# Grouped instance normalisation in 4 MB tiles: statistics by sum and square instead of BN_STATS, coefficients for pairs of tiles

## The chip, the cores and the metric

The kernel runs on one core of one Trainium2 chip. The metric is device time in microseconds (us), the median of several executions of the whole kernel. For the kernel before it is 634.74 us over 12 runs, from 634.29 to 635.12 us.

Five engines of the core matter here. TensorE (PE) does small matrix products, VectorE (DVE) and ScalarE (ACT) do the work on the data, GpSimd (POOL) sets up constants, and SyncE (SP) only issues transfers. Transfers are carried by 16 DMA engines that all queues share.

## The reference

```python
B, G, C_per_g, H, W = 4, 8, 16, 256, 256
def reference(x, gamma):
    mu = x.mean(axis=(3, 4), keepdims=True)
    var = ((x - mu) ** 2).mean(axis=(3, 4), keepdims=True)
    x_norm = (x - mu) / np.sqrt(var + 1e-5)
    out = x_norm * gamma[None, :, :, None, None]
    return out.astype(np.float32)
```

There are 4 x 8 x 16 = 512 channels of 65,536 float32 numbers each. Every channel gets its own mean and variance, and every number of it becomes `x * scale + shift`, with scale = gamma / sqrt(var + 1e-5) and shift = -mean * scale. All of x has to be read before its channel can be written. In all 134.22 MB are read and 134.22 MB are written.

## The kernel before

**Units.** A channel is cut into S = 4 rows of F = 16384 numbers, and each row lies in one partition, so 128 partitions hold K = 32 channels: a unit of 8 MB. There are U = 16 units. A unit is loaded as two tiles (NCK = 2) of 128 x 8192 numbers, 4 MB each; in memory the rows of a tile are 32 KB long and start 64 KB apart. The pool `data` has six tiles (line 40), so three units are resident.

**Loads.** `load(u)` (lines 47 to 53) issues both transfers of a unit on SyncE's queue. Units 0 and 1 are loaded at once (line 55), unit u + 1 at the head of the loop's pass u. A load into a tile that has been used waits on SyncE until the store of that tile's old content is complete.

**Statistics.** `stats(u)` runs 32 BN_STATS of 512 columns on VectorE (line 94). `finalize` (lines 100 to 133) joins them with one BN_AGGREGATE (line 102), makes mean and mean square per partition, averages the four partitions of each channel with a matrix product on TensorE against the constant `avg` (line 109), and then makes nmean, var, std (Sqrt on ScalarE, line 125), rstd, scale and shift (lines 114 to 132), each a small instruction on 128 partitions.

**Normalising and storing.** `emit` (lines 135 to 141) normalises each of the two tiles in place on ScalarE (line 138) and issues its store on ScalarE's queue (line 141).

**Order.** The order is written out by hand: `manual_schedule` leaves each engine's instructions as the program lists them, and each engine works its own list in order, waiting on semaphores where its data comes from elsewhere. The loop is

```python
st0 = stats(0)
for u in range(1, U):
    if u + 1 < U:
        tiles[u + 1] = load(u + 1)
    st = stats(u)
    if u == 1:
        emit(0, *finalize(0, st0))
    emit(u, *finalize(u, st))
```

so `finalize(0)` stands behind `stats(1)` in VectorE's list, and in every later pass a unit's statistics, coefficients and stores follow each other.

Of the kernel before, what the change touches and what calls it, by code (L numbers as in the profile page):

```python
# [1 line left out]

# [4 lines left out]

F32 = mybir.dt.float32
ALU = mybir.AluOpType
ACTF = mybir.ActivationFunctionType  # L10


@with_exitstack
def kernel(
    ctx: ExitStack,
    tc: tile.TileContext,
    x: bass.AP,
    gamma: bass.AP,
    out: bass.AP,
):  # L20
    nc = tc.nc
    B, G, C, H, W = x.shape
    P = nc.NUM_PARTITIONS
    HW = H * W
    n_ch = B * G * C
    S = 4
    K = P // S
    F = HW // S
    U = n_ch // K
    CW = 8192  # L30
    NCK = F // CW
    FMAX = 512
    NG = (G * C) // K
    assert HW % S == 0 and F % CW == 0 and (G * C) % K == 0

    xv = x.rearrange("b g c h w -> (b g c h w)").rearrange("(u p f) -> u p f", p=P, f=F)
    ov = out.rearrange("b g c h w -> (b g c h w)").rearrange("(u p f) -> u p f", p=P, f=F)
    gv = gamma.rearrange("g c -> (g c)")

    data = ctx.enter_context(tc.tile_pool(name="data", bufs=3 * NCK))  # L40
    singles = ctx.enter_context(tc.tile_pool(name="singles", bufs=1))
    stats_pool = ctx.enter_context(tc.tile_pool(name="stats", bufs=2))
    psum = ctx.enter_context(tc.tile_pool(name="psum", bufs=2, space=bass.MemoryType.PSUM))

    ctx.enter_context(tc.manual_schedule())

    def load(u):
        ts = []
        for j in range(NCK):
            t = data.tile([P, CW], F32, name="xt")  # L50
            nc.sync.dma_start(out=t[:], in_=xv[u, :, j * CW : (j + 1) * CW])  # L51
            ts.append(t)
        return ts

    tiles = {0: load(0), 1: load(1)}


    g_row = singles.tile([1, G * C], F32, name="g_row")
    nc.scalar.dma_start(out=g_row[:], in_=gv[None, :])
    eps_t = singles.tile([P, 1], F32, name="eps_t")  # L60
    nc.vector.memset(eps_t[:], 1e-5)  # L61
    avg = singles.tile([P, K, S], F32, name="avg")
    nc.gpsimd.memset(avg[:], 1.0 / S)  # L63
    nc.gpsimd.affine_select(  # L64
        out=avg[:], in_=avg[:], pattern=[[-S, K], [0, S]], compare_op=ALU.is_ge,
        fill=0.0, base=0, channel_multiplier=1,
    )
    nc.gpsimd.affine_select(  # L68
        out=avg[:], in_=avg[:], pattern=[[S, K], [0, S]], compare_op=ALU.is_ge,
        fill=0.0, base=S - 1, channel_multiplier=-1,  # L70
    )
    one = singles.tile([1, 1], F32, name="one")
    nc.vector.memset(one[:], 1.0)
    g_rep = singles.tile([1, NG, K, S], F32, name="g_rep")
    nc.vector.tensor_copy(  # L75
        out=g_rep[:],
        in_=g_row[:].rearrange("o (n k) -> o n k", n=NG).unsqueeze(3).to_broadcast([1, NG, K, S]),
    )
    g_ps = psum.tile([P, NG], F32, name="g_ps")
    for n in range(NG):  # L80
        nc.tensor.matmul(  # L81
            out=g_ps[:, n : n + 1],
            lhsT=g_rep[:, n].rearrange("o k s -> o (k s)"),
            rhs=one[:],
            start=True, stop=True,
        )
    g_col = singles.tile([P, NG], F32, name="g_col")
    nc.vector.tensor_copy(out=g_col[:], in_=g_ps[:])  # L88

    def stats(u):  # L90
        st = stats_pool.tile([P, F // FMAX, 6], F32, name="st")
        for j in range(NCK):
            for s in range(CW // FMAX):
                nc.vector.bn_stats(  # L94
                    out=st[:, j * (CW // FMAX) + s, :],
                    in_=tiles[u][j][:, s * FMAX : (s + 1) * FMAX],
                )
        return st

    def finalize(u, st):  # L100
        mv = stats_pool.tile([P, 2], F32, name="mv")
        nc.vector.bn_aggr(out=mv[:], in_=st[:].rearrange("p n s -> p (n s)"))  # L102

        nc.vector.scalar_tensor_tensor(  # L104
            out=mv[:, 1:2], in0=mv[:, 0:1], scalar=mv[:, 0:1], in1=mv[:, 1:2],
            op0=ALU.mult, op1=ALU.add,
        )
        ps = psum.tile([P, 2], F32, name="ps")
        nc.tensor.matmul(  # L109
            out=ps[:], lhsT=avg[:].rearrange("p k s -> p (k s)"), rhs=mv[:],  # L110
            start=True, stop=True,
        )
        cm = stats_pool.tile([P, 2], F32, name="cm")
        nc.vector.tensor_copy(out=cm[:], in_=ps[:])  # L114
        nmean = stats_pool.tile([P, 1], F32, name="nmean")
        nc.vector.tensor_scalar(  # L116
            out=nmean[:], in0=cm[:, 0:1], scalar1=-1.0, scalar2=None, op0=ALU.mult,
        )
        var = stats_pool.tile([P, 1], F32, name="var")
        nc.vector.scalar_tensor_tensor(  # L120
            out=var[:], in0=cm[:, 0:1], scalar=nmean[:], in1=cm[:, 1:2],
            op0=ALU.mult, op1=ALU.add,
        )
        std = stats_pool.tile([P, 1], F32, name="std")
        nc.scalar.activation(out=std[:], in_=var[:], func=ACTF.Sqrt, bias=eps_t[:], scale=1.0)  # L125
        rstd = stats_pool.tile([P, 1], F32, name="rstd")
        nc.vector.reciprocal(out=rstd[:], in_=std[:])  # L127
        scale = stats_pool.tile([P, 1], F32, name="scale")
        g = u % NG
        nc.vector.tensor_mul(out=scale[:], in0=rstd[:], in1=g_col[:, g : g + 1])  # L130
        shift = stats_pool.tile([P, 1], F32, name="shift")
        nc.vector.tensor_mul(out=shift[:], in0=nmean[:], in1=scale[:])  # L132
        return scale, shift

    def emit(u, scale, shift):
        for j in range(NCK):
            t = tiles[u][j]
            nc.scalar.activation(  # L138
                out=t[:], in_=t[:], func=ACTF.Identity, bias=shift[:], scale=scale[:],
            )  # L140
            nc.scalar.dma_start(out=ov[u, :, j * CW : (j + 1) * CW], in_=t[:])


    st0 = stats(0)
    for u in range(1, U):
        if u + 1 < U:
            tiles[u + 1] = load(u + 1)
        st = stats(u)
        if u == 1:
            emit(0, *finalize(0, st0))  # L150
        emit(u, *finalize(u, st))
        del tiles[u - 1]


# [1 line left out]
_INS = ['x', 'gamma']  # L156
_OUTS = [((4, 8, 16, 256, 256), 'float32')]


# [23 lines left out]
```

## Time and profile before

| what | value |
|---|---|
| median of 12 runs | 634.74 us |
| the profiled execution's own time | 634.29 us |
| its span, first to last instruction | 632.6 us |
| VectorE busy | 343.3 us (54%), 644 instructions |
| ScalarE busy | 236.8 us (37%), 49 instructions |
| TensorE busy | 11.2 us (2%) |
| DMA, all queues | 268.50 MB, mean 424 GB/s over the span |
| one load, from issue to landing, median | 27.4 us |
| one store, from issue to landing, median | 50.7 us |

The page cuts the span into 40 equal slices of 15.8 us. A digit is the busy share of an engine in the slice in tenths, 9 meaning 90% or more; below it stands what the DMA engines moved. Queue q1 carries the loads issued by SyncE, q10 the stores issued by ScalarE, and q14 carries transfers of instructions. A group line names the source line, the engine, the operation, what is written and read, and how often; then busy time in us and mean ns of one; then the engine's idle time just before these instructions and what ended it. A suffix q (ACTq, SPq) marks the sequencer of an engine, which issues transfers without keeping the engine busy.

### The profile page before, as it was taken

How to read it: one execution, taken by the hardware profiler on the slowest of the kernel's cores; microseconds unless marked ns; L12 is line 12 of the kernel's file. 1: busy time of each engine (PE TensorE's matmuls, PEld its weight loads, DVE VectorE, ACT ScalarE, POOL GpSimd, SP SyncE). 2: the span in 40 equal slices, each digit the busy share in tenths (PEclk: the TensorE clock that was granted, in tenths of full speed). 3: DMA queues.
4: the chain of work that ended last, by engine and by line, in shares of the span. 5: the costliest groups of instructions: out<-in, count | busy, mean ns of one | idle time of the engine just before them, and what ended most of it. 6: DMA issues, size and time to landing. Idle time of an engine off the chain costs nothing.

```text
span 632.6 us, 972 instructions
## 1 busy us (share of the span) xinstructions
PE 11.2 (2%) x40; PEld 9.8 (2%) x40; DVE 343.3 (54%) x644; ACT 236.8 (37%) x49; POOL 1.4 (0%) x7
## 2 busy tenths in 40 slices
PE   1000000000000000000000000000000000000000
PEld 1000000000000000000000000000000000000000
DVE  2995486454765536665356653467535575354700
ACT  0004958053170622607135080440904408053180
POOL 0000000000000000000000000000000000000000
DMA  8998999999999999999999999999999999999996
GB/s 369 439 438 346 398 425 431 435 431 429 433 431 431 431 433 431 433 434 436 435 437 431 437 431 435 432 431 431 431 431 431 433 433 440 439 431 433 433 431 278
DMA packets 9226, 268.50 MB, mean 424 GB/s; under 512 B 1026, under 2 KB 1027, under 8 KB 1027
## 3 DMA queue, kind: packets, MB, share of 16 engines
q1 hardware_dynamic: 4608, 134.22, 49.4%
q10 hardware_dynamic: 4610, 134.22, 49.3%
q14 instruction: 8, 0.06, 0.0%
HBM read 134.22 MB, written 134.22 MB: 424 GB/s over the span
## 4 chain that ended last, share of the span: by engine, by line
DMA 60%; DVE 17%; another core or an unknown queue 12%; ACT 7%; PE 1%; issue 1%; SPq 0%; ACTq 0%
DMA xt<-in_x_dram 41%; DMA out_dram<-xt 19%; DVE st L94 14%; ACT xt L138 7%; DVE mv L102 1%; PE ps L109 1%; SPq L51 0%; DVE mv L104 0%; DVE var L120 0%; ACT std L125 0%; DVE cm L114 0%; DVE nmean L116 0%; DVE rstd L127 0%; DVE shift L132 0%
## 5 line engine op out<-in xcount | busy, mean ns | idle before, releaser
L94 DVE BATCH_NORM_STATS2 st<-xt 128x6 f32<-128x512 f32 x512 | 306.8, 677 | 219.4 <-DMA xt<-in_x_dram 219.2
L138 ACT ACTIVATE xt<-xt,shift,scale 128x8192 f32<-128x8192 f32 x32 | 230.8, 7213 | 16.7 <-DVE shift L132 9.9
L125 ACT ACTIVATE std<-var,eps_t 128x1 f32<-128x1 f32 x16 | 4.7, 295 | 359.6 <-DVE var L120 359.1
L109 PE MATMUL ps<-mv,avg 128*128 128x2 f32 x32 | 9.4, 362 | 584.2 <-DVE mv L104 584.2
L109 PEld LDWEIGHTS ps<-mv,avg 128*128 128x128 f32 x32 | 8.0, 311 | 585.5 <-DVE mv L104 536.1
L102 DVE BATCH_NORM_AGGREGATE mv<-st 128x2 f32<-128x192 f32 x16 | 16.3, 1021 | 0.5
L127 DVE RECIPROCAL rstd<-std 128x1 f32<-128x1 f32 x16 | 2.6, 164 | 18.6 <-ACT std L125 18.6
L114 DVE COPY cm<-ps 128x2 f32<-128x2 f32 x16 | 2.5, 159 | 10.9 <-PE ps L109 10.9
L120 DVE SCALAR_TENSOR_TENSOR var<-cm,nmean 128x1 f32<-128x1 f32 x16 | 3.5, 220 | 0.6
L104 DVE SCALAR_TENSOR_TENSOR mv<-mv 128x1 f32<-128x1 f32 x16 | 3.5, 219 | 0.6
L132 DVE TENSOR_TENSOR shift<-nmean,scale 128x1 f32<-128x1 f32 x16 | 2.6, 160 | 0.6
L130 DVE TENSOR_TENSOR scale<-rstd,g_col 128x1 f32<-128x1 f32 x16 | 2.5, 159 | 0.5
L116 DVE TENSOR_SCALAR nmean<-cm 128x1 f32<-128x1 f32 x16 | 2.5, 154 | 0.6
L81 PE MATMUL g_ps<-one,g_rep 1*128 1x1 f32 x8 | 1.9, 350 | 2.5 <-DVE g_rep L75 2.5
L81 PEld LDWEIGHTS g_ps<-one,g_rep 1*128 1x128 f32 x8 | 1.8, 322 | 2.5 <-DVE g_rep L75 2.5
L125 ACT ACT_TABLE_LOAD x1 | 1.3, 1283 | 1.3 <-PEq L167 1.3
L88 DVE COPY g_col<-g_ps 128x4 f32<-128x4 f32 x1 | 0.2, 162 | 2.0 <-PE g_ps L81 2.0
L75 DVE COPY g_rep<-g_row 1x512 f32<-1x512 f32 x1 | 0.4, 414 | 1.1 <-DMA g_row<-in_gamma_dram 1.1
L61 DVE MEMSET eps_t<- 128x1 f32 x1 | 0.1, 59 | 0.9 <-PEq L167 0.9
L64 POOL TENSOR_SCALAR_AFFINE_SELECT avg<-avg 128x128 f32<-128x128 f32 x1 | 0.5, 520 | 0.1
L68 POOL TENSOR_SCALAR_AFFINE_SELECT avg<-avg 128x128 f32<-128x128 f32 x1 | 0.5, 519 | 0.1
L63 POOL MEMSET avg<- 128x128 f32 x1 | 0.2, 205 | 0.3 <-POOLq L167 0.3
(5 smaller groups left out, 0.5 us busy)
## 6 DMA issues: line engine op xcount, KB each, us to landing
xt<-in_x_dram SPq DMA_DIRECT2D x32, 4096.0 KB, 27.4
out_dram<-xt ACTq DMA_DIRECT2D x32, 4096.0 KB, 50.7
g_row<-in_gamma_dram ACTq DMA_DIRECT2D x1, 0.5 KB
```

The lines of the kernel that those rows point to most:

```text
L81: nc.tensor.matmul(out=g_ps[:, n : n + 1], lhsT=g_rep[:, n].rearrange("o k s -> o (k s)"), rhs=one[:], start=True, stop=True,)
L94: nc.vector.bn_stats(out=st[:, j * (CW // FMAX) + s, :], in_=tiles[u][j][:, s * FMAX : (s + 1) * FMAX],)
L102: nc.vector.bn_aggr(out=mv[:], in_=st[:].rearrange("p n s -> p (n s)"))
L104: nc.vector.scalar_tensor_tensor(out=mv[:, 1:2], in0=mv[:, 0:1], scalar=mv[:, 0:1], in1=mv[:, 1:2], op0=ALU.mult, op1=ALU.add,)
L109: nc.tensor.matmul(out=ps[:], lhsT=avg[:].rearrange("p k s -> p (k s)"), rhs=mv[:], start=True, stop=True,)
L114: nc.vector.tensor_copy(out=cm[:], in_=ps[:])
L116: nc.vector.tensor_scalar(out=nmean[:], in0=cm[:, 0:1], scalar1=-1.0, scalar2=None, op0=ALU.mult,)
L120: nc.vector.scalar_tensor_tensor(out=var[:], in0=cm[:, 0:1], scalar=nmean[:], in1=cm[:, 1:2], op0=ALU.mult, op1=ALU.add,)
L125: nc.scalar.activation(out=std[:], in_=var[:], func=ACTF.Sqrt, bias=eps_t[:], scale=1.0)
L127: nc.vector.reciprocal(out=rstd[:], in_=std[:])
L132: nc.vector.tensor_mul(out=shift[:], in0=nmean[:], in1=scale[:])
L138: nc.scalar.activation(out=t[:], in_=t[:], func=ACTF.Identity, bias=shift[:], scale=scale[:],)
```

## The change

The unit becomes one tile: S = 8 rows of 8192 numbers per channel, K = 16 channels, U = 32 units of 4 MB, each contiguous in memory and moved by one transfer. Six tiles are resident as before, and all six are loaded at the start.

The statistics are a sum per partition on VectorE (`reduce_sum`) and a sum of squares on ScalarE (Square with an accumulator output; the squares themselves go to a byte tile `junk` that nobody reads). A matrix product with `navg` (-1/HW within each channel's eight partitions) gives minus the mean and minus the mean square in PSUM. Coefficients are made for two units together; the last two units are handled one by one. Of a pair, the first unit is normalised on VectorE and the second on ScalarE; of the last two units, 5376 columns on VectorE and 2816 on ScalarE. Stores stay on ScalarE's queue, after both normalisations of the pair, and each is followed in the program by the load of the unit six further on.

The diff, cut to its core; the constants' set-up moves from VectorE to GpSimd, and gamma is spread over eight columns instead of four.

```diff
-    S = 4
+    S = 8
...
-    CW = 8192
-    NCK = F // CW
-    FMAX = 512
     NG = (G * C) // K
+    AHEAD = 6
+    DV = 5376
...
-    data = ctx.enter_context(tc.tile_pool(name="data", bufs=3 * NCK))
+    data = ctx.enter_context(tc.tile_pool(name="data", bufs=AHEAD))
...
     def load(u):
-        ts = []
-        for j in range(NCK):
-            t = data.tile([P, CW], F32, name="xt")
-            nc.sync.dma_start(out=t[:], in_=xv[u, :, j * CW : (j + 1) * CW])
-            ts.append(t)
-        return ts
+        t = data.tile([P, F], F32, name="xt")
+        nc.sync.dma_start(out=t[:], in_=xv[u])
+        tiles[u] = t
-    tiles = {0: load(0), 1: load(1)}
+    for u in range(AHEAD):
+        load(u)
...
+    junk = singles.tile([P, F], U8, name="junk")
...
+    def coefficients(lo, n):
+        hi = lo + n
+        for u in range(lo, hi):
+            t = tiles[u]
+            nc.vector.reduce_sum(out=st[:, u, 0:1], in_=t[:], axis=AX.X)
+            nc.scalar.activation(
+                out=junk[:], in_=t[:], func=ACTF.Square, accum_out=st[:, u, 1:2],
+            )
+        ps = psum.tile([P, n, 2], F32, name="ps")
+        nc.tensor.matmul(
+            out=ps[:].rearrange("p n c -> p (n c)"), lhsT=navg_w,
+            rhs=st[:, lo:hi].rearrange("p n c -> p (n c)"), start=True, stop=True,
+        )
+        for i in range(n):
+            nc.vector.tensor_scalar(
+                out=nvar[:, lo + i : lo + i + 1], in0=ps[:, i, 0:1], scalar1=ps[:, i, 0:1],
+                scalar2=ps[:, i, 1:2], op0=ALU.mult, op1=ALU.add,
+            )
+        nc.scalar.activation(
+            out=std[:, lo:hi], in_=nvar[:, lo:hi], func=ACTF.Sqrt, bias=eps_t[:], scale=-1.0,
+        )
+        nc.vector.reciprocal(out=rstd[:, lo:hi], in_=std[:, lo:hi])
+        g = lo % NG
+        nc.vector.tensor_mul(out=scale[:, lo:hi], in0=rstd[:, lo:hi], in1=g_col[:, g : g + n])
+        nc.vector.tensor_mul(out=shift[:, lo:hi], in0=ps[:, :, 0], in1=scale[:, lo:hi])
+
+    def norm_vector(u, a, b):
+        t = tiles[u]
+        nc.vector.tensor_scalar(
+            out=t[:, a:b], in0=t[:, a:b], scalar1=scale[:, u : u + 1],
+            scalar2=shift[:, u : u + 1], op0=ALU.mult, op1=ALU.add,
+        )
+
+    def norm_scalar(u, a, b):
+        t = tiles[u]
+        nc.scalar.activation(
+            out=t[:, a:b], in_=t[:, a:b], func=ACTF.Identity,
+            bias=shift[:, u : u + 1], scale=scale[:, u : u + 1],
+        )
+
+    def store(u):
+        nc.scalar.dma_start(out=ov[u], in_=tiles.pop(u)[:])
...
+    for u in range(0, U - 2, 2):
+        coefficients(u, 2)
+        norm_vector(u, 0, F)
+        norm_scalar(u + 1, 0, F)
+        for v in (u, u + 1):
+            store(v)
+            if v + AHEAD < U:
+                load(v + AHEAD)
+    for u in range(U - 2, U):
+        coefficients(u, 1)
+        norm_vector(u, 0, DV)
+        norm_scalar(u, DV, F)
+        store(u)
```

## The prediction

> **What bounds the kernel now.** I read the page first, then the waits of the load queue, then the DMA share in short windows round every slice where it drops, and last the order of time on ScalarE's queue at both ends.
>
> ```profile
> span 632.6 us, 972 instructions
> ...
> DMA  8998999999999999999999999999999999999996
> GB/s 369 439 438 346 398 425 431 435 431 429 433 431 431 431 433 431 433 434 436 435 437 431 437 431 435 432 431 431 431 431 431 433 433 440 439 431 433 433 431 278
> ...
> q1 hardware_dynamic: 4608, 134.22, 49.4%
> q10 hardware_dynamic: 4610, 134.22, 49.3%
> ...
> L94 DVE BATCH_NORM_STATS2 st<-xt 128x6 f32<-128x512 f32 x512 | 306.8, 677 | 219.4 <-DMA xt<-in_x_dram 219.2
> L138 ACT ACTIVATE xt<-xt,shift,scale 128x8192 f32<-128x8192 f32 x32 | 230.8, 7213 | 16.7 <-DVE shift L132 9.9
> ```
>
> The DMA engines are the bound: loads (q1) and stores (q10) together occupy 98.7% of 16 engines' span, 624.4 us for 64 transfers, so 9.76 us for one of 4 MB. Each engine gets 128/16 = 8 of its 32 KB packets, 1.22 us each. VectorE (54%) and ScalarE (37%) wait. The rate falls below 420 only in slices 0, 3 and 4 and in the last one; only there is anything to win.
>
> ```profile
> SPq L51 <- DMA out_dram<-xt: 545.4, 26, 70.6
> ```
>
> Nearly all of SyncE's time is a wait for a store to free a tile: the six tiles are always full, and a load goes out when a store ends.
>
> ```profile
> 59.00:60.00 1.00, 0.00 (x0) 0.00 (x0) 0.00 (x0) 1.00 (x1) 0.00 (x0) 1.00 1.15 492
> 60.00:61.00 1.00, 0.00 (x0) 0.00 (x0) 0.00 (x0) 1.00 (x1) 0.00 (x0) 1.00 0.16 66
> 61.00:62.00 1.00, 0.00 (x0) 0.00 (x0) 0.00 (x0) 1.00 (x1) 0.00 (x0) 1.00 0.00 0
> 62.00:63.00 1.00, 0.00 (x0) 0.00 (x0) 0.00 (x0) 1.00 (x1) 0.00 (x0) 1.00 0.00 0
> 63.00:64.00 1.00, 0.00 (x0) 0.00 (x0) 0.00 (x0) 0.54 (x2) 0.00 (x0) 1.00 0.08 33
> ```
>
> The last two columns are DMA share and GB/s; a packet is booked in the window where it starts. All six first loads are in by about 60.8, and nothing moves until the first store, about 64.0: a hole. Of the 4 us after 60, 0.24 us of packets start and about 0.6 us run over from before, so about 3.1 us are empty.
>
> ```profile
> 63.11 0.38 ACTq L141 DMA_DIRECT2D out_dram<-xt  x1
> ...
> 606.76 0.34 ACTq L141 DMA_DIRECT2D out_dram<-xt  x1
> ...
> 614.45 0.34 ACTq L141 DMA_DIRECT2D out_dram<-xt  x1
> ```
>
> The first store is late because L94 sums units 0 and 1, four tiles, before finalize(0) runs. At the other end the last stores are issued at 606.8 and 614.5, while the share is 0.99 from 608 to 626: older stores still run, so the last unit's work is hidden already.
>
> ```profile
> 626.00:627.00 1.00, 0.00 (x0) 0.00 (x0) 0.00 (x0) 0.00 (x0) 0.00 (x0) 1.00 0.76 328
> 627.00:628.00 1.00, 0.00 (x0) 0.00 (x0) 0.00 (x0) 0.00 (x0) 0.00 (x0) 1.00 0.08 33
> 628.00:629.00 1.00, 0.00 (x0) 0.00 (x0) 0.00 (x0) 0.00 (x0) 0.00 (x0) 1.00 0.08 33
> 629.00:630.00 1.00, 0.00 (x0) 0.00 (x0) 0.00 (x0) 0.00 (x0) 0.00 (x0) 1.00 0.08 33
> ```
>
> One packet on one engine is 1.22/16 = 0.08. So 15 engines start their last packets before 627 (most end near 627.3), and one engine alone starts three more and ends at 630.7: it is 3.4 us behind. The cause offered: of queue q14, instruction fetches, the trace has five packets of 8 KB between 62 and 627 us:
>
> ```profile
> q14 instruction: 5, 0.04, 0.0%
> ```
>
> 3.4/5 is about 0.7 us each, if most sit on that one engine (an inference, not read off a row).
>
> **The Trainium skill.** "DMA: Bandwidth & Descriptors", section "Issuing engines are not separate DMA queues": all queues share the same 16 engines and interleave. The trace agrees: a load needs 27.4 us in the median beside stores, against 9.76 us of packet time. Same page, "Where 436 GB/s comes from": a ceiling of 435.2 GB/s. The trace shows 433 between 100 and 560 us, so making the rows contiguous has nothing to win. "Runtime: NRT & Kernel Launch", "Instruction fetch mechanics": a sequencer fetches its instructions through a DMA queue of its own, so the number of instructions matters. It speaks of 16 KiB blocks; the trace has packets of 8 KB, and I count with those.
>
> **The change part by part.** The bytes, the 64 transfers, the 128 x 32 KB rows and the six tiles stay: 624.4 us of packets stay.
>
> *Statistics.* Out: 512 BN_STATS (9.6 us a tile) and 16 aggregations. In: per tile one VectorE sum and one ScalarE square over 128x8192. No row shows the sum; "VectorE: DVE Perf Modes", "The perf-mode tier table", gives tensor_reduce one element a cycle whatever the type, so 8192/0.96 GHz plus overhead = 8.7 us (estimate); bounds 4.4 (were it two a cycle) and 9.6 (today's). The square has L138's shape, so 7.2 us; an accumulator output and the byte-typed junk are not shown, bounds 7.2 and 14.4 (double); I take 7.2. The VectorE normalise: the same table has fp32 tensor_scalar at two a cycle (1227 ns for 2048), so 4.4 us; bounds 4.4 and 8.7. The coefficient chain: matmul 0.6, two small VectorE steps 0.4, Sqrt 0.3, three more 0.5, hops 0.4 = 2.2 us, once per pair; today's chain is 3.5 us. A second table load, 1.3 us by the row of today's one (1283 ns), is issued after the first pair's VectorE step, once.
>
> Per pair VectorE works 2 x 8.7 + 4.4 + 0.9 = 22.7 us, ScalarE 2 x 7.2 + 0.3 + 7.2 = 21.9 us; the pair's four transfers take 4 x 9.76 = 39.0 us. All of it lies beside DMA: cost nothing. With the upper bounds: VectorE 28.8, ScalarE 36.3, still below 39.0.
>
> *First store.* Tile 0 lands at 13.0 (first BN_STATS), tile 1 9.7 later at 22.7; sum to 31.4; chain 2.2 + 1.3 to 34.9; ScalarE's normalise to 42.1; store issued about 42.5, not 63.1. The loads in flight last to 60.8, so 18 us of cover: the hole goes, **-3.1 us** on 15 of 16 engines. Even 14.4 us squares would only bring the store to about 50.
>
> *Steady state.* Loads lead by the time they ran alone, from about 2 to 43.4 us, 4.2 transfers; then both queues take turns. A pair whose second tile lands at T has stores ready at T + 8.7 + 2.2 + 7.2 + 0.4 = T + 18.5. At T some four stores are left in the queue, two of them this pair's own, so the queue has two transfers before it, 39 us at half rate: 20 us in hand. ScalarE's store u+4 also waits for store u's completion (eight DMA semaphores; the same wait stands in today's order); behind it on ScalarE's queue are the next pair's squares. That store ended 18 us or more before: nothing. Load v+6 waits on SyncE for store v, as today; one more load is always queued ahead.
>
> *End.* When the last load lands, about 4.2 stores remain, 41 us. The last unit needs 8.7 + 2.2 + 2.9 (5376 columns on VectorE, 2816 on ScalarE beside it) + 0.9 to the first packet = 15 us, under the 31 us of stores ahead of its own. The split DV thus buys nothing; without that cover it would cost these 15 us.
>
> *Instruction fetches.* VectorE falls from 644 instructions, about a fetch per 128, to 136 in the order of the changed kernel; ScalarE rises to 103 plus waits. I expect one to two fetches in place of six. The late engine then lags 0.7 to 1.4 us plus up to 1 us from the start that the hole swallows today. I take 1.0 (0 to 3.4 as bounds).
>
> *Sum, in the profiled execution.* Most engines end at 627.3 - 3.1 = 624.2; late engine +1.0 = 625.2; from the last packet to the span's end 1.9 as now (632.6 - 630.7) = 627.1; outside the span 1.7 (634.29 - 632.58) = 628.8. The profiled run is 0.45 below the median 634.74, so **629.3 us**.
>
> **Rivals.** (a) *The lag stays*: fetches don't follow the instruction count, or the late engine is slow for another reason. For it: only five packets, placed by inference. Against: nothing else in the profile distinguishes one engine. Only the hole goes: 634.74 - 3.1 = 631.6.
> (b) *The hole moves*: loads lead less, and a later pair finds the store queue empty. For it: tiles now wait in pairs and one ScalarE does squares and normalising. Against: 20 us in hand. It would return the 3 us: about 634.7.
> (c) *ScalarE becomes the bound, slower than before*: the squares, in every pair. The period reaches the DMA's 39.0 us from (39.0 - 7.2 - 0.3 - 1.8)/2 = 14.9 us a square, with 1.8 us of waits; the loss begins near 14 us, when the last units are no longer covered. At 16 us: 13 + 15 x 41.3 + 2 x 22 + 10 = 687 us. For it: no row shows an accumulating square. Against: it needs twice L138's duration for the same elements.
>
> **How the numbers follow.** Forecast 0.78 (628.0 to 630.9 from the bounds of the lag and about 0.5 us of slow packets where stores set in); (a) 0.13 (630.9 to 633.4); (b) 0.04; (c) 0.05. The range 627.6 to 632.4 holds the forecast and most of (a). A measurement of this kernel can tell about 0.2% (1.3 us) from no change: 0.91 faster, 0.04 same, 0.05 slower.
>
> **What would show it.** Right: first store issued at 40 to 45 us; DMA share near 1 in every window from 3 to 624 us; at most four instruction packets; the last load landing about 40 us before the end; the lone engine's tail under two packets. Wrong: a square over 13 us, a hole in the middle, packets above 1.22 us (contiguous rows slower), or three lone packets again at the end.

## The result and the profile after

The changed kernel takes 643.46 us (median of 7 runs, 640.86 to 644.15) against 634.80 us before: ratio 1.0131, 95% interval 1.0121 to 1.0140. It is 1.3% slower, where 629.3 us was forecast and 632.4 us was the upper end of the range. The profiled execution, the shortest of the seven, took 640.86 us with a span of 639.1 us. Where some runs of a kernel lie more than 1.5% above its fastest, the ratios below leave those runs out, and the medians keep them.

The page of the changed kernel, in the order of the lines shown of before:

```profile
span 639.1 us, 570 instructions
...
DMA  9999999999999999999999999999999999999996
GB/s 375 441 400 441 429 408 422 422 429 427 425 423 429 420 435 429 409 435 414 433 435 412 433 412 429 433 418 425 422 431 429 418 431 418 431 427 420 433 433 269
...
q1 hardware_dynamic: 4608, 134.22, 50.4%
q10 hardware_dynamic: 4610, 134.22, 48.7%
q14 instruction: 3, 0.02, 0.0%
...
L103 DVE TENSOR_REDUCE st<-xt 128x1 f32<-128x8192 f32 x32 | 277.8, 8685 | 214.8 <-DMA xt<-in_x_dram 214.8
L104 ACT ACTIVATE junk<-xt 128x8192 uint8<-128x8192 f32 x32 | 224.9, 7030 | 204.3 <-DMA xt<-in_x_dram 203.5
```

The DMA digits are 9 up to the last slice: the engines are busy throughout, and yet they move less, 400 to 441 GB/s between the first slice and the last, with many dips. The two queue lines say where. The loads (q1) occupied 50.4% of 639.1 us = 322.1 us of each engine, before 49.4% of 632.6 = 312.5 us; the stores (q10) 311.2 us, before 311.9. The same 4096 packets of 32 KB that carry the loads took 10 us longer per engine. VectorE and ScalarE wait for loads as before (214.8 and 203.5 us).

The hole is gone, as forecast. Short windows round 61 us (the last two columns are DMA share and GB/s):

```profile
58.00:60.00 2.00, 0.00 (x0) 0.00 (x0) 1.53 (x5) 1.20 (x2) 0.00 (x0) 1.00 0.80 344
60.00:62.00 2.00, 0.00 (x0) 0.00 (x0) 2.00 (x1) 2.00 (x1) 0.00 (x0) 1.00 1.22 524
62.00:64.00 2.00, 0.00 (x0) 0.00 (x0) 2.00 (x2) 2.00 (x1) 0.00 (x0) 1.00 0.96 410
```

What took its place shows in windows of 4 us in the steady state:

```profile
118.00:122.00 4.00, 0.00 (x0) 0.00 (x0) 1.92 (x1) 1.86 (x1) 0.00 (x0) 1.00 1.07 459
122.00:126.00 4.00, 0.00 (x0) 0.00 (x0) 4.00 (x1) 4.00 (x1) 0.00 (x0) 1.00 0.96 360
126.00:130.00 4.00, 0.56 (x2) 0.50 (x2) 3.25 (x3) 1.26 (x2) 0.00 (x0) 1.00 1.06 459
```

From 122 to 126 us the share is 0.96 and the rate 360: 375 GB/s per unit of share, where its neighbours have 430. A packet there takes longer; no engine is idle. In the packet records of the trace (which give start, duration and queue of each packet) nearly all 32 KB packets take 1.213 us; the slow ones are load packets of 1.25 to 2.46 us, 509 of the 4096, and four in five of them lie in the second and third of the eight that each engine moves of a load. There is such a cluster about every 20 us, at each load that runs beside stores. ("Slow load packets, us per engine" is from here on the sum of what load packets took beyond 1.213 us, divided by 16.)

At the end the DMA engines no longer finish together:

```profile
630.00:631.00 1.00, 0.00 (x0) 0.00 (x0) 0.00 (x0) 0.00 (x0) 0.00 (x0) 1.00 1.06 459
631.00:632.00 1.00, 0.00 (x0) 0.00 (x0) 0.00 (x0) 0.00 (x0) 0.00 (x0) 1.00 0.53 229
632.00:633.00 1.00, 0.00 (x0) 0.00 (x0) 0.00 (x0) 0.00 (x0) 0.00 (x0) 1.00 0.53 229
...
636.00:637.00 1.00, 0.00 (x0) 0.00 (x0) 0.00 (x0) 0.00 (x0) 0.00 (x0) 1.00 0.23 98
```

One engine is 0.08 of share, so about three are still at work after 636. In the packet records the engines end at 633.6 us on the mean and at 637.8 at the latest. (The records don't name the engine; a packet starts where the one before it on its engine ends, and the packets were joined to 16 chains by that.)

When do the clusters come? The first store, and then the landings against the issues of loads. ScalarE's queue, changed kernel:

```profile
35.01 7.21 ACT L134 ACTIVATE xt<-xt,shift,scale 128x8192 f32<-128x8192 f32 x1 [0.68 <-DVE shift L123]
39.53 3.06 ACTq L140 DMA_DIRECT2D out_dram<-xt  x2
```

The first store is issued at 39.5 us, while ScalarE is still normalising unit 1 (until 42.2): although it stands behind both normalisings in the program, it waits only for VectorE's half of the pair. In the steady state, VectorE's order of time (a sum starts as its tile lands) and SyncE's (a load goes out as a store completes):

```profile
120.08 8.69 DVE L103 TENSOR_REDUCE st<-xt 128x1 f32<-128x8192 f32 x1 [10.90 <-DMA xt<-in_x_dram]
```

```profile
124.55 39.96 SPq L50 DMA_DIRECT2D xt<-in_x_dram  x3
```

A load lands and the next begins at about 120, and 4.5 us later a store is complete and the following store has begun. In the kernel before the same two rows are 10.7 us apart:

```profile
119.85 9.59 DVE L94 BATCH_NORM_STATS2 st<-xt 128x6 f32<-128x512 f32 x16 [9.77 <-DMA xt<-in_x_dram]
```

```profile
130.60 20.29 SPq L51 DMA_DIRECT2D xt<-in_x_dram  x2
```

From the packet records: in the changed kernel a store's first packets start 2.5 to 4.7 us after those of a load (medians of the 16 engines), in the kernel before 12.1 us from the fourth store on, and there nearly every packet takes 1.213 us. This time from the start of a load to the start of a store is called the distance below. In the changed kernel it is 2.5 to 2.9 us at first and wanders up to 4.7 as the run goes on. That distance became the first theory.

### The profile page after: what moved, and what is told of

The parts are those of the page before. It is cut to its first block, busy times and chain, and to the rows that moved or that the text cites. A ratio compares the mean times of both kernels' runs of the same rounds, so it can differ in the third digit from the quotient of the medians.

```text
span 639.1 us, 570 instructions
## 1 busy us (share of the span) xinstructions
PE 13.1 (2%) x50; PEld 12.0 (2%) x50; DVE 369.0 (58%) x134; ACT 349.2 (55%) x100; POOL 1.3 (0%) x9
## 3 DMA queue, kind: packets, MB, share of 16 engines
q1 hardware_dynamic: 4608, 134.22, 50.4%
## 4 chain that ended last, share of the span: by engine, by line
DMA 68%; DVE 12%; another core or an unknown queue 12%; ACT 2%; PE 1%; issue 0%; SPq 0%; ACTq 0%
DMA out_dram<-xt 36%; DMA xt<-in_x_dram 32%; DVE st L103 8%; DVE xt L127 3%; ACT xt L134 1%; PE ps L108 1%; DVE nvar L113 0%; SPq L50 0%; ACT std L117 0%; ACT L117 0%; DVE rstd L120 0%; DVE scale L122 0%; DVE shift L123 0%; ACTq L134 0%
## 5 line engine op out<-in xcount | busy, mean ns | idle before, releaser
L103 DVE TENSOR_REDUCE st<-xt 128x1 f32<-128x8192 f32 x32 | 277.8, 8685 | 214.8 <-DMA xt<-in_x_dram 214.8
L104 ACT ACTIVATE junk<-xt 128x8192 uint8<-128x8192 f32 x32 | 224.9, 7030 | 204.3 <-DMA xt<-in_x_dram 203.5
L134 ACT ACTIVATE xt<-xt,shift,scale 128x8192 f32<-128x8192 f32 (+1 forms) x17 | 113.7, 6686 | 11.6 <-DVE shift L123 11.6
L127 DVE TENSOR_SCALAR xt<-xt,scale,shift 128x8192 f32<-128x8192 f32 (+1 forms) x17 | 74.4, 4374 | 0.9 <-DVE shift L123 0.3
L117 ACT ACTIVATE std<-nvar,eps_t 128x2 f32<-128x2 f32 (+1 forms) x17 | 5.0, 296 | 42.4 <-DVE nvar L113 42.4
L108 PE MATMUL ps<-st,navg 128*128 128x4 f32 (+1 forms) x34 | 9.5, 351 | 591.7 <-DVE st L103 566.9
L108 PEld LDWEIGHTS ps<-st,navg 128*128 128x128 f32 x34 | 8.5, 310 | 592.7 <-issue 567.8
L113 DVE TENSOR_SCALAR nvar<-ps 128x1 f32<-128x1 f32 x32 | 7.8, 283 | 12.8 <-PE ps L108 12.8
L120 DVE RECIPROCAL rstd<-std 128x2 f32<-128x2 f32 (+1 forms) x17 | 2.8, 166 | 7.5 <-ACT std L117 7.5
L104 ACT ACTIVATION_READ_ACCUMULATOR junk<-xt 128x1 f32 x32 | 6.0, 186 | 0.0
```

The lines of the kernel that those rows point to most:

```text
L103: nc.vector.reduce_sum(out=st[:, u, 0:1], in_=t[:], axis=AX.X)
L104: nc.scalar.activation(out=junk[:], in_=t[:], func=ACTF.Square, accum_out=st[:, u, 1:2],)
L108: nc.tensor.matmul(out=ps[:].rearrange("p n c -> p (n c)"), lhsT=navg_w, rhs=st[:, lo:hi].rearrange("p n c -> p (n c)"), start=True, stop= ...
L113: nc.vector.tensor_scalar(out=nvar[:, lo + i : lo + i + 1], in0=ps[:, i, 0:1], scalar1=ps[:, i, 0:1], scalar2=ps[:, i, 1:2], op0=ALU.mult, ...
L117: nc.scalar.activation(out=std[:, lo:hi], in_=nvar[:, lo:hi], func=ACTF.Sqrt, bias=eps_t[:], scale=-1.0,)
L120: nc.vector.reciprocal(out=rstd[:, lo:hi], in_=std[:, lo:hi])
```

## The experiments

Theories at the start: *phase* (the distance in time between the start of a load and the start of a store decides, and the first store sets it for the whole run), *compute* (VectorE and ScalarE both reading the landed tile slow the load in progress), *addresses* (tiles contiguous in memory). Every run is compared with runs of the kernel before on the same chip.

**Shift the first store by 2 us.**

```diff
+    spare = singles.tile([P, 1], F32, name="spare")
...
         coefficients(u, 2)
+        if u == 0:
+            nc.vector.reduce_sum(out=spare[:], in_=tiles[0][:, 0:1792], axis=AX.X)
         norm_vector(u, 0, F)
```

> The changed kernel with one extra VectorE sum over 1792 columns (about 1.9 us, result unused) ahead of the first pair's normalising, so that the first store starts about 2 us later in the course of the fifth load. In the trace of the changed kernel the slow load packets (11.6 us per DMA engine in all) fall where a store begins about 2.7 us after a load. Theory phase (the two queues change transfers too close together, and the first store sets for the whole run how far apart): stores now begin near the middle of a load, the slow packets go, about 629 us. Theory compute (VectorE and ScalarE both reading the tile just landed slow the load that is running): stays near 643 us. Theory addresses (tiles contiguous in memory, against 64 KB row pitch): stays near 643 us.

Measured: 627.14 us (627.05 to 627.45), ratio 0.9882 (0.9865 to 0.9898). Two microseconds of useless work took off 16 us. In the packet records a store now begins 7.2 us after a load, and the slow load packets cost 1.6 us per engine instead of 11.3.

**No engine work after the first pair.**

```diff
+        W = F if lo == 0 else 64
...
-            nc.vector.reduce_sum(out=st[:, u, 0:1], in_=t[:], axis=AX.X)
+            nc.vector.reduce_sum(out=st[:, u, 0:1], in_=t[:, 0:W], axis=AX.X)
...
-        norm_vector(u, 0, F)
-        norm_scalar(u + 1, 0, F)
+        N = F if u == 0 else 64
+        norm_vector(u, 0, N)
+        norm_scalar(u + 1, 0, N)
...
```

> The changed kernel with the first pair as it is, and from the second pair on sums, squares and normalising over 64 columns only (nearly all statistics and normalising are left out; all transfers stay, in the same order, and the first store starts as before). Theory compute: the slow load packets go, about 629 us. Theory phase and theory addresses: near 643 us, the slow packets again in the second and third of eight rounds of each load.

Measured: 642.81 us (641.98 to 643.57), ratio 1.0127 (1.0111 to 1.0142); distance 2.8 to 4.7 us, slow load packets 10.6 us per engine. With VectorE and ScalarE all but idle the loss is the same. Theory compute falls.

**The kernel before, first store early, at two moments.**

```diff
-    st0 = stats(0)
-    for u in range(1, U):
-        if u + 1 < U:
-            tiles[u + 1] = load(u + 1)
+    tiles[2] = load(2)
+    for u in range(U):
         st = stats(u)
-        if u == 1:
-            emit(0, *finalize(0, st0))
         emit(u, *finalize(u, st))
-        del tiles[u - 1]
+        if u + 3 < U:
+            tiles[u + 3] = load(u + 3)
+        del tiles[u]
```

> The kernel before with unit 0 finalised and stored ahead of the statistics of unit 1: first store issued at about 43 us, no empty stretch before it; row pitch 64 KB and BN_STATS as before. Its first store should begin near the middle of a load. Theories phase, compute and addresses: all 3 us below the kernel before, about 631.6 us (the late engine keeps its five instruction fetches).

Measured: 631.15 us (630.93 to 631.25), ratio 0.9943 (0.9928 to 0.9958), distance 9.6 us. The 3.6 us that it gains are not simply the hole. The empty 3.1 us per engine at 61 us are gone, but the last unit now leaves a new gap, 2.8 us per engine, between 600 and 608 us:

```profile
600.00:605.00 5.00, 0.00 (x0) 0.00 (x0) 0.00 (x0) 5.00 (x1) 0.00 (x0) 1.00 0.70 301
605.00:610.00 5.00, 0.00 (x0) 0.00 (x0) 0.00 (x0) 4.53 (x2) 0.00 (x0) 1.00 0.75 321
```

On the mean the engines end only 1.1 us earlier (626.5 and 627.6). The late engine makes up most of its lag in the new gap: the last engine is 1.0 us behind the mean in place of 3.1. Together that is the 3.2 us between the spans (632.6 and 629.4).

For the second moment VectorE gets ten BN_STATS more ahead of the first coefficients:

```diff
+        if u == 0:
+            spare = stats_pool.tile([P, 10, 6], F32, name="spare")
+            for s in range(10):
+                nc.vector.bn_stats(out=spare[:, s, :], in_=tiles[0][1][:, s * FMAX : (s + 1) * FMAX])
```

> The same with ten extra BN_STATS (6 us, results unused) ahead of the first finalize: the first store then begins about 3 us after the start of a load, the distance seen in the changed kernel. Theory phase: slow load packets appear, 638 to 645 us, with the addresses and the engine work of the kernel before. Theories compute and addresses: about 631.6 us, as without the extra work.

Measured: 632.24 us (632.17 to 632.54), ratio 0.9961 (0.9946 to 0.9976). It doesn't decide: the store began so late in the sixth load that the next load had to wait for it, which moved the distance to 9.7 us. The bad distance came once, at the first store (3.1 us).

**The old addresses at the bad distance, two ways.** First the changed kernel with the tiles of a pair as the two halves of 64 KB rows:

```diff
-        nc.sync.dma_start(out=t[:], in_=xv[u])
+        nc.sync.dma_start(out=t[:], in_=xv[u // 2, :, (u % 2) * F : (u % 2 + 1) * F])
...
```

The stores follow suit, and a pair now makes up one unit of 32 channels with one set of coefficients, the last pair too.

> The changed kernel with the addresses of the kernel before: units of 32 channels x 4 partitions again, each the two tiles of a pair, rows 32 KB long at a 64 KB pitch; sums, squares, pairs, split of the normalising and order as in the changed kernel, first store at the same moment (first packet near 44.3 us). Theory phase: about 643 us with slow load packets, since the stores still begin about 3 us after a load. Theory addresses: about 627 us without them.

Measured: 662.97 us (656.77 to 665.39), ratio 1.0433 (1.0378 to 1.0488). The distance is 2.4 to 3.6 us up to 250 us and is then lost. Slow load packets cost 6.8 us per engine, and stores are slow as well (13.8 us). From 620 to 639 us, besides, only four of the sixteen engines are at work:

```profile
625.00:630.00 5.00, 0.00 (x0) 0.00 (x0) 5.00 (x1) 5.00 (x1) 0.00 (x0) 1.00 0.24 105
```

The other twelve stand empty until the next store, which waits for the coefficients of the last pair, made from both its tiles, and is issued at 637.8 us. So the old addresses don't take the slow packets away; how much of the longer time is theirs and how much comes with the last pair isn't separated. Then the kernel before, in the order with the early store (as in the run with 631.15 us):

```diff
-            for s in range(CW // FMAX):
+            for s in range(CW // FMAX - (5 if u == 0 and j == 1 else 0)):
...
```

> The kernel before with unit 0 stored ahead of the statistics of unit 1, and with the last five BN_STATS of unit 0 left out (unit 0's mean and variance then come from 27 of 32 pieces), so that the first store is issued near 39.6 us as in the changed kernel. Theory phase: slow load packets with the addresses, the BN_STATS and the engine work of the kernel before, 640 to 647 us. Theory addresses: 631 us, as without the omission.

Measured: 642.77, 645.73, 684.99 and 685.65 us, against 634.6 before. In the profiled one (645.73) the distance is 2.8 to 4.8 us and the slow load packets cost 12.0 us per engine in place of 1.7; its stores, at the same 64 KB pitch, are not slow (0.5 us). Its span is 14.6 us longer than with the early store alone (644.0 and 629.4): about 10.3 are the slow packets, and about 4.7 a longer gap near 615 us (7.5 us per engine in place of 2.8). Why two of the runs took 685 us no trace shows. So the kernel before, with its own addresses, BN_STATS and engine work, becomes slower than it was when its first store moves to the moment of the changed kernel's. Theory addresses, as first put, falls.

**Other distances.** The first store comes later than the changed kernel's by more useless work (4608 elements, shown here) or by less (768, in the third of these runs), and earlier by handing a part of VectorE's first normalising to ScalarE:

```diff
+    spare = singles.tile([P, 1], F32, name="spare")
...
+        if u == 0:
+            nc.vector.reduce_sum(out=spare[:], in_=tiles[0][:, 0:4608], axis=AX.X)
         norm_vector(u, 0, F)
```

> As the run with the 1.9 us delay, with a sum over 4608 columns (4.9 us): the first store begins near the end of the fifth load, so that later on a store begins 13 to 16 us after a load, 3 to 6 us ahead of the next one. Theory phase in its plain form (near means near, on either side): between 627 us and 643 us, with slow packets. If only a store shortly after a load is bad: 627 us.

Measured: 627.14 us (627.01 to 627.31), ratio 0.9884 (0.9869 to 0.9898), distance 12.1 us.

```diff
-        norm_vector(u, 0, F)
+        if u == 0:
+            norm_vector(u, 0, DV)
+            norm_scalar(u, DV, F)
+        else:
+            norm_vector(u, 0, F)
```

> The changed kernel with the first unit's normalising split over both engines, so that the first store is issued about 1.6 us earlier (37.9 us) and later stores begin within about 1 us of a load. Theory phase: 640 to 648 us, slow packets as before or more. If exact coincidence is harmless and only a distance of some 3 us is bad: near 627 us.

Measured: 627.89 us (627.53 to 630.26), ratio 0.9903 (0.9884 to 0.9922), distance 0.8 to 1.1 us: near coincidence is nearly harmless. The plain form of theory phase (near is bad) falls; what is left is a bad stretch.

> As the delayed runs, with a sum over 768 columns (about 0.95 us): stores begin about 4.5 to 5.5 us after a load, between the bad 2.7 to 4.7 us of the changed kernel and the good 7.2 us. Theory distance: 627 to 643 us; it places the upper edge of the bad stretch. No theory says below 627.

Measured: 629.92 us median of 629.43, 629.48, 630.36 and 644.38, ratio 0.9921 (0.9904 to 0.9937); distance 4.8 us in the profiled run (629.43), without clusters of slow packets there (1.6 us per engine). This is the edge.

> The changed kernel with the first unit's normalising split over both engines at 6784 columns, the first store issued about 0.8 us earlier: stores begin some 1.5 to 2.5 us after a load, between the good 1 us and the bad 2.7 us. Theory distance: 628 to 643 us; it places the lower edge.

(6784 in place of DV.) Measured: 632.11 us, but from 627.28 to 656.40 in twelve runs; distance 1.2 us in the profiled run. The lower edge doesn't hold still from one execution to the next.

**The same shift without extra work.** For the first pair the engines are exchanged:

```diff
-        norm_vector(u, 0, F)
-        norm_scalar(u + 1, 0, F)
+        if u == 0:
+            norm_scalar(u, 0, F)
+            norm_vector(u + 1, 0, F)
+        else:
+            norm_vector(u, 0, F)
+            norm_scalar(u + 1, 0, F)
```

> The changed kernel without extra work, with the engines of the first pair exchanged: unit 0 is normalised on ScalarE (7.2 us) and unit 1 on VectorE (4.4 us), so that the first store is issued near 42.3 instead of 39.5 us and a store begins some 7 to 9 us after a load. Theory distance (slow packets only where a store begins about 3 to 5 us after a load, found so far good at 1, 7, 10 and 12 us): 627.1 us, no slow packets. If the extra VectorE work and not the later first store helped in the delayed runs: 643 us.

Measured: 627.14 us (627.07 to 627.97), ratio 0.9883 (0.9867 to 0.9900). This version beats both kernels. Its page and its steady state:

```profile
span 625.4 us, 569 instructions
...
q1 hardware_dynamic: 4608, 134.22, 49.9%
q10 hardware_dynamic: 4610, 134.22, 49.7%
```

```profile
42.25 0.84 ACTq L140 DMA_DIRECT2D out_dram<-xt  x2
```

```profile
116.55 8.69 DVE L103 TENSOR_REDUCE st<-xt 128x1 f32<-128x8192 f32 x1 [10.69 <-DMA xt<-in_x_dram]
```

```profile
125.93 39.04 SPq L50 DMA_DIRECT2D xt<-in_x_dram  x3
```

The first store leaves at 42.25, 2.7 us later than in the changed kernel. From landing to the next load's issue there are now 9.4 us in place of 4.5 (a store begins 7.3 us after a load in the packet records), and the loads take 49.9% of 625.4 = 312.1 us of each engine, 10 us less.

**The late engine.** Many small instructions in the kernel with the 2 us delay:

```diff
         norm_scalar(u + 1, 0, F)
+        if u > 0:
+            for _ in range(36):
+                nc.vector.memset(spare[:], 0.0)
```

> The run with the 1.9 us delay, plus 36 VectorE memsets of one column after each later pair's normalising (504 instructions, results unused, VectorE still under 30 us of the 39 us per pair). Theory fetch (each block of instructions that VectorE fetches holds up one DMA engine by about 0.7 us): four more instruction packets, one engine late by about 3 us, 630 us. If the late engine of the kernel before has another cause: 627.1 us.

Measured: 630.60 us (630.47 to 630.83), ratio 0.9934 (0.9920 to 0.9949), 3.5 us more than without them. Its page and its last windows:

```profile
q14 instruction: 7, 0.06, 0.0%
```

```profile
622.00:623.00 1.00, 0.00 (x0) 0.00 (x0) 0.00 (x0) 0.00 (x0) 0.00 (x0) 1.00 0.53 229
623.00:624.00 1.00, 0.00 (x0) 0.00 (x0) 0.00 (x0) 0.00 (x0) 0.00 (x0) 1.00 0.16 66
624.00:625.00 1.00, 0.00 (x0) 0.00 (x0) 0.00 (x0) 0.00 (x0) 0.00 (x0) 1.00 0.08 33
625.00:626.00 1.00, 0.00 (x0) 0.00 (x0) 0.00 (x0) 0.00 (x0) 0.00 (x0) 1.00 0.08 33
626.00:627.00 1.00, 0.00 (x0) 0.00 (x0) 0.00 (x0) 0.00 (x0) 0.00 (x0) 1.00 0.08 33
```

With seven instruction packets in place of three (the changed kernel's number; the run without the memsets has three too), one engine alone is late again by three packets, as in the kernel before. By itself this doesn't show that the fetches make it late, for the distance moved too: it is 5.1 us here and 7.2 without the memsets. At 4.8 us, in the run with the short delay, one engine alone is late as well, with three packets of instructions:

```profile
q14 instruction: 3, 0.02, 0.0%
```

```profile
623.00:624.00 1.00, 0.00 (x0) 0.00 (x0) 0.00 (x0) 0.00 (x0) 0.00 (x0) 1.00 0.08 33
624.00:625.00 1.00, 0.00 (x0) 0.00 (x0) 0.00 (x0) 0.00 (x0) 0.00 (x0) 1.00 0.00 0
625.00:626.00 1.00, 0.00 (x0) 0.00 (x0) 0.00 (x0) 0.00 (x0) 0.00 (x0) 1.00 0.08 33
```

It ends at 626.4, the next engine at 624.2. There the lag grows little by little: the last packet of a load is 1.2 us behind the median of the last sixteen at 60 us and 3.4 us behind at 410, with no step at the fetches (180 and 214 us).

The kernel before shows the fetches' part better. There the last packet of a store is 0.3 us behind the median of the last sixteen at 129 us and then, in steps, 0.8, 1.6, 2.5 and 2.9 us behind. The steps follow fetches at 143, 280, 397 and 522 us (one at 300 leaves none), and between them the lag stands still; the run with the early store has steps after its fetches at 279, 396 and 521 us too. So in these two runs one engine loses 0.4 to 0.9 us where a fetch falls, but an engine can also fall behind without fetches.

**Why is that distance bad?** Four runs, none of which found the cause. Loads in two transfers of 64 partitions each:

```diff
-        nc.sync.dma_start(out=t[:], in_=xv[u])
+        for h in range(0, P, P // 2):
+            nc.sync.dma_start(out=t[h : h + P // 2], in_=xv[u, h : h + P // 2])
```

> The run with the 4.9 us delay (a store begins 12.1 us after a load, 627.1 us), with each load issued as two transfers of 64 partitions: same bytes, same 32 KB packets, but a second load transfer begins 9.7 us into each tile, so a store begins about 2.4 us after that. Theory transfer start (it is the start of any load transfer shortly ahead of a store's that is bad): slow load packets again, 632 to 650 us. Theory tile (only the first rows of a tile matter, or the landing): 627 us.

> Control: the same halved loads in the kernel with the first pair's engines exchanged, where a store begins 7.3 us after a load and 2.4 us ahead of the second half's start. Both theories: about 627 us, unless the halves cost by themselves, which would show here.

Measured: 785.89 us (781.36 to 790.88), ratio 1.2384 (1.2314 to 1.2454), and for the control 781.77 us (772.68 to 804.74), ratio 1.2270 (1.2189 to 1.2350). The control is as slow, so the pair says nothing on the transfer's start. It says something else: with only loads in progress the engines are busy at half the rate. The control's windows, before any store:

```profile
10.00:20.00 10.00, 0.00 (x0) 0.00 (x0) 0.00 (x0) 0.00 (x0) 0.00 (x0) 1.00 1.01 210
20.00:30.00 10.00, 0.00 (x0) 0.00 (x0) 6.18 (x1) 6.20 (x2) 0.00 (x0) 1.00 0.98 203
```

The unhalved kernel has 442 and 423 GB/s in these windows.

Loads from other addresses, at the distance of the changed kernel:

```diff
-        nc.sync.dma_start(out=t[:], in_=xv[u])
+        nc.sync.dma_start(out=t[:], in_=xv[0])
```

> The changed kernel with every load reading the first 4 MB of the input (so every unit holds unit 0's data; all transfers, engine work and moments as before). Theory addresses read against addresses written: the relation changes from unit to unit, the slow packets change with it, well below 643 us. If the addresses don't matter: 643 us as in the changed kernel.

Measured: 643.25 us (642.95 to 644.94), ratio 1.0142 (1.0125 to 1.0159).

```diff
-        nc.sync.dma_start(out=t[:], in_=xv[u])
+        at = min(u * P * F + F // 2, (U - 1) * P * F)
+        nc.sync.dma_start(out=t[:], in_=xf[at : at + P * F].rearrange("(p f) -> p f", f=F))
```

> The changed kernel with every load but the last reading from 16 KB further on (units hold data shifted by 4096 numbers; all else the same). Theory addresses: at other offsets the slow packets become fewer or more, below 638 or above 650 us. If the addresses don't matter: 643 us.

Measured: 643.24 us (640.90 to 644.02), ratio 1.0129 (1.0108 to 1.0149). Neither moves the time: which rows are read while which are written doesn't matter for contiguous tiles.

The distances together, from the packet records of the profiled runs; the time is the median, with the range where it is wide:

| run | store after load, us | slow load packets, us per engine | time, us |
|---|---|---|---|
| near coincidence | 0.8 to 1.1 | 1.7 | 627.9 |
| lower edge | 1.2 | 1.9 | 632.1 (627.3 to 656.4) |
| changed kernel | 2.5 to 4.7 | 11.3 | 643.5 |
| before, store at the changed kernel's moment | 2.8 to 4.8 | 12.0 | 642.8 to 685.7; this one 645.7 |
| upper edge | 4.8 | 1.6 | 629.9 (629.4 to 644.4) |
| 2 us delay and memsets | 5.1 | 1.8 | 630.6 |
| 2 us delay; engines exchanged | 7.2; 7.3 | 1.6; 1.5 | 627.1; 627.1 |
| before, store early | 9.6 | 1.7 | 631.2 |
| 5 us delay | 12.1 | 1.6 | 627.1 |

The table doesn't give the bad stretch an exact width. In the runs with many slow packets the distance is 2.4 to 3.3 us at the second and third store and wanders from there, so a distance of 3.5 to 4.7 us was never set on purpose. The two edges (1.2 and 4.8 us in the profiled runs) are slow in some executions and not in others.

## Why the prediction was wrong, by its steps

- **"The bytes, the 64 transfers, the 128 x 32 KB rows and the six tiles stay: 624.4 us of packets stay." This step failed.** Bytes and packets stayed, their time didn't: together they took 633.3 in place of 624.4 us per engine, loads 322.1 in place of 312.5. The packet time was read off a kernel whose two queues happen to start their transfers 12.1 us apart, and was taken for a property of the bytes. The same term sets the end: against the version with the engines exchanged the engines end 10.4 us later on the mean (633.6 and 623.2), and the latest is 4.2 us behind the mean in place of 0.9. Together 13.7 us, the difference of the spans 639.1 and 625.4.
- **"First store"** had a second, smaller error that decided the sign. It put the first store at 42.5 us, after ScalarE's normalising; it left at 39.5, since it waits for VectorE alone and ScalarE's queue issues it beside the running ACTIVATE. At 42.3 us (engines exchanged) the kernel takes 627.1 us. "Even 14.4 us squares would only bring the store to about 50" asked only whether the store would be late, never whether its moment sets the order of the queues.
- **The hole**: it went, as forecast. The early store in the kernel before gains 3.6 us, but that this is near the 3.1 us forecast is chance, since 2.1 of the 3.2 us between the spans are the late engine's lag. The version with the engines exchanged supports the size: its engines end 4.4 us earlier on the mean than in the kernel before (623.2 and 627.6), 1.3 us of that is shorter packet time (623.2 and 624.4 us per engine), and 3.1 remain.
- **The instruction fetches**: right in kind, not in all. One to two were expected and three came. The forecast lag of 1.0 us is what the version with the engines exchanged has (0.9 behind the mean); in the changed kernel itself the slow packets set the end. The kernel before shows the steps of the lag at its fetches, but the runs at distances of 0.8 to 1.2, 4.8 and 5.1 us have late engines again, and all but the last of them have three fetches. The Trainium skill ("Runtime: NRT & Kernel Launch", "Instruction fetch mechanics") says that a sequencer fetches through a DMA queue of its own; the trace agrees so far as that instructions come on q14, apart from loads and stores, and has packets of 8 KB.
- **Engine work beside DMA**: right. Sum 8.69 us (8.7), square 7.03 with 0.19 for reading the accumulator (7.2), VectorE's normalise 4.55 (4.4), first chain 3.5 with the table load (3.5). The run with next to no engine work after the first pair takes as long (642.81 us), so none of it is on the path there.
- **The sum**: for the kernel that it described, one without slow packets, 629.3 us was 2.2 us too high: the last engine ended at 624.1, not 625.2 (1.1 us); from the last packet to the end of the span it took 1.3, not 1.9 (0.6); and the profiled run was not 0.45 below the median. The range of the forecast doesn't follow from its bounds: a lag of 0 to 3.4 us alone gives 628.3 to 631.7, not 628.0 to 630.9.
- **Rivals**: none was it. (b) didn't come, and (a), one lagging engine as before, is not what made this kernel slower: three engines end together at 637.8; (c), ScalarE as the bound, was refuted by the 7.03 us squares. The list of signs did have "packets above 1.22 us (contiguous rows slower)": the sign came, for another reason, since the kernel before has slow packets too at this distance, with its 64 KB pitch.

The explanation rests on this: moving the first store by 2 to 3 us, by useless work or by exchanging engines, removes the slow load packets and the loss, and moving it the other way in the kernel before creates them. That is shown. What inside the DMA engines makes a distance of some 2.5 to 4.7 us bad stays open; engine work after the first pair and the addresses read are ruled out.

## What to carry to other kernels

In these kernels, bound by DMA with one load queue and one store queue of equal transfers, the moment of the first store set how the two queues interleave for nearly the whole run. It was worth 16 us of 640 in the changed kernel, and 11.6 us or more the other way in the kernel before (631.15 against 642.77 and up). If packets in the trace last longer than the commonest duration with all engines busy, compare the start times of transfers on the two queues, and shift the first store by a few microseconds before changing anything else. A DMA share of 1 isn't a rate: divide the GB/s by the share.

## What the runs showed of the hardware

- Most load packets of 32 KB last 1.213 us. Where a store starts some 2.5 to 4.7 us after a load, 509 of 4096 last 1.25 to 2.46 us; with the engines exchanged (7.3 us) 44 do so. Slow store packets cost 0.6 us per engine in the changed kernel and 13.8 in its form with the 64 KB pitch.
- A queue that started beside a busy one waited: the changed kernel's first store was issued at 39.5 us and its first packet began at 44.3, 4.8 us later; in the kernel before, with no other traffic, it took 0.9 us (63.1 to 64.0).
- Loads of 64 partitions, queued behind each other and with all 16 engines busy, run at 203 to 210 GB/s, half of the 423 to 442 of 128 partitions.
- In the kernel before one DMA engine falls behind by 0.4 to 0.9 us after fetches of 8 KB of instructions (at 143, 280, 397 and 522 us).
- A store on ScalarE's queue is issued while an earlier ACTIVATE of that engine still runs, if it doesn't wait for it.
